# Input weights in tile slots, a second buffer for the decay factors, and reorderings in the merge, cross-attention and second feed-forward product of a hybrid decoder block

## The chip, the cores and the metric

The kernel runs on one core of a Trainium2 chip. The metric is the device time of one execution in microseconds. A core has a matmul engine (PE, with a queue of its own for loading weights, PEld), a vector engine (DVE), a scalar engine (ACT), a third elementwise engine (POOL), a queue that issues most DMAs (SP) and 16 DMA engines that these transfers share. Each engine carries out its own list of instructions strictly in order and waits on semaphores for the others; an instruction that waits holds up everything behind it on its engine.

## The reference, cut to what matters

```python
u = rms_norm(x, norm_mix)                                  # 1024 tokens x 1024
u_ssm, q, k, v, f, gates = split(u @ w_in)
y  = gelu(s5_ssm(u_ssm, lam_re, lam_im, log_dt, b_re, b_im, c_re, c_im, d_skip))
a, b = split(y @ w_glu);  out_a = a * sigmoid(b)
out_b = forgetting_attention(q, k, v, f + b_forget) @ w_fox_o
ga, gb = split(sigmoid(gates))
h = x + (ga * out_a + gb * out_b) @ w_mix_out              # the merge of the branches
h = h + memory_cross_attention(rms_norm(h), rms_norm(mem), w_mem_q, w_mem_kv, w_mem_o)
fa, fb = split(rms_norm(h) @ w_ffn_in)                     # 2 x 2816 columns
h = h + (silu(fa) * fb) @ w_ffn_out
return rms_norm(h, norm_final)

def s5_ssm(u, ...):                                        # 32 groups x 64 complex states
    dt = exp(log_dt);  lam_bar = exp(lam * dt);  b_bar = (lam_bar - 1) / lam * b
    states = scan(s[t] = lam_bar * s[t-1] + b_bar @ u[t])
    return real(c @ states) + d_skip * u
```

All inputs and results are float32.

## The kernel before, in words

**Precision and tiles.** Every float32 operand of a matmul is split into a high part (an ACT cast, `A.copy`, line 178) and a low part (a subtraction on DVE or POOL, line 179); a product is three matmuls of high and low parts (lines 168 to 170). Tiles have 128 partitions. An accumulator occupies a bank: there are tags `mm`, `sc`, `pv` and `misc`, and `misc` has one buffer, so whoever fills it next waits until the one before has been read by both the ACT cast and the DVE subtraction.

**stage_in.** The x tiles (0 to 7) and the memory tiles (m, n) are loaded into 11 slots of the tag `xt`, normalised, turned by PE through banks misc and pv (line 226), and split on the way out (`E` steps; `uh`, `ul` for x). Weights are loaded (`D`, line 388), split (`W`) and used: W0 to W3 are keys, W4 to W7 values, W8 to W11 (written 8, 9, a, b in the table) the 512 columns of the input projection for the state-space branch (`U`), whose splits also rearrange columns. The order is the table `ORDER_IN`, one step after the other; within it a scheduler places every engine's instructions, so the lists of the engines are not simply the table cut in five. Raw weights have 4 slots. The keys and values (`kv`) are stored to `kv_d` right after they are made (lines 412 and 427), and the projected columns to `u_d` (line 439).

**stage_ssm.** The 16 column blocks of the gates (24 matmuls for each half, then a sigmoid on ACT, line 475, and a store) fill PE while DVE, POOL and ACT prepare the state-space products of four quarters q. Per quarter: POOL and DVE build tables (`w`, `Gm`, the doubled rotations `EC`, `ES`); ACT copies the decay factors into `r` (line 1354); DVE runs two scans with `r` (lines 1414 and 1415, `zre` and `zim`); a Toeplitz table `Ts` is completed by three DMAs that shift it (line 1378) and copied to `Tt` (line 1383); PE then multiplies `Tt` and the states `St` (lines 1442 and 1443). Gate weights come two blocks at a time, p = 0 to 7, each as two 512 KB loads (`raw`, line 153).

**Merge.** `fox_part` multiplies the attention by `w_fox_o` into pv banks, multiplies by gate `gb` (line 538) and adds; the result is split and goes through `w_mix_out` (`mix`).

**Cross-attention.** For each half of the heads and block of tokens: `mem_scores` (scores, exponent, normalising on POOL, `pe`, line 697), `mem_turn` (PE turns the probabilities, line 706), `mem_values`. `mem_turn` of one block follows the scores of the next.

**Feed-forward.** Both products use a scheme with seven products of half-size blocks instead of eight (names A11, A12, A22, S1 to S4). The first runs over 22 column blocks j: `start`, `middle`, `end` are PE work (line 878), `w_first`, `w_sums` and `w_last` split the weights; `middle` ends with an ACT copy `c` (line 899) of bank mm, which PE needs next for S4. The second product reads operands of 128 x 1024 (`or`), fetched and split by `o_get` seven steps ahead of `o_mm`; the first few are split while the last block of the first product runs.

**Order.** `with B.behind(i)` puts the instructions in its body behind instruction `i` in the list of their own engines; it adds no wait between engines.

Of the kernel before, what the change touches and what calls it, by code (L numbers as in the profile page):

```python
# [66 lines left out]
def f32(ap):  # L67
    return ap.bitcast(F32)
# [50 lines left out]
class Block:  # L119
# [57 lines left out]
    def split(self, hi, lo, src, pool_lo=False):  # L177
        self.A.copy(hi, src)  # L178
        (self.G if pool_lo else self.V).tensor_sub(lo, src, f32(hi))  # L179

    def rstd(self, src):
# [47 lines left out]
    def turned(self, ps, b, act, t):  # L229
        for i in range(0, 4, act.kg):  # L230
            hi, lo = act.tok(4 * b + i, t, act.kg)
            self.split(hi, lo, ps[:, i * P:(i + act.kg) * P].rearrange("p (k c) -> p k c", k=act.kg))

# [104 lines left out]
def stage_in(B, xp, s5, x, mem, g_mix, g_kv, w_in, w_mem_kv, uT, u_d, kv_d):  # L338
# [7 lines left out]
    mT = Act(xp, "mT", 4, 8, ML, kg=4, name="m")  # L346
    tiles, gain, ss, rs, raw, w, ps, us, kv = {}, {}, {}, {}, {}, {}, {}, [], []
    names = {"m": -2, "n": -1, **{str(t): t for t in range(NT)}}
# [28 lines left out]
    def evac(t, b):  # L377
        B.turned(ps.pop((t, b)), b, *((mT, t + 2) if t < 0 else (uT, t)))

    def wget(i):  # L380
        if i < 4:
            src = w_mem_kv[:, i * P:(i + 1) * P]
        elif i < 8:
            src = w_mem_kv[2 * (i - 4) * P:2 * (i - 3) * P, 512:1024]
        else:
            src = w_in[:, C_U + (i - 8) * P:C_U + (i - 7) * P]
        raw[i] = B.wpool.tile([P, RAW], F32, tag="raw", bufs=4, name="raw")[:, :D]
        S.dma_start(raw[i].rearrange("p (k c) -> p k c", k=D // src.shape[-1]),
                    src.rearrange("(k p) c -> p k c", p=P))
# [15 lines left out]
    def keys_out(h):  # L405
        if not kv:
            kv.extend(xp.tile([P, D], F32R, tag="kv", bufs=4, name="kv") for _ in range(4))
        cs = slice(h * ML, (h + 1) * ML)
        B.split(kv[0][:, cs], kv[1][:, cs], ps.pop(("k", h))[:, :ML])
        if h == 3:  # L410
            for i in range(2):
                S.dma_start(kv_d[i], f32(kv[i]))

# [8 lines left out]
    def values_out():  # L422
        for t in range(2):
            cs = slice(t * 512, (t + 1) * 512)
            B.split(kv[2][:, cs], kv[3][:, cs], ps.pop(("v", t)))
        for i in range(2, 4):
            S.dma_start(kv_d[i], f32(kv[i]))
# [5 lines left out]
    def ssm_out(q, h):  # L433
# [4 lines left out]
        if h == 1:  # L438
# [9 lines left out]
            "K": lambda a: keys(int(a)), "k": lambda a: keys_out(int(a)), "V": lambda a: values(int(a)),  # L448
            "v": lambda a: values_out(), "U": lambda a: ssm_in(int(a[0]), int(a[1])),
            "u": lambda a: ssm_out(int(a[0]), int(a[1])), "L": lambda a: s5.load(int(a)),  # L450
# [5 lines left out]
def stage_ssm(B, s5, qp, uT, w_in, gate_d, u_d, y_d):  # L456
# [5 lines left out]
    def gate_weights(p):  # L462

        w[p] = [B.wblock(w_in, 4 * n, 4, C_G + 256 * p, 256) for n in range(2)]

# [38 lines left out]
def stage_tail(B, big, s2, sh, x, glu, aT, gate_d, kv_d, w_fox_o, w_mix_out, g_mq, w_mem_q, w_mem_o, g_ffn,  # L504
# [21 lines left out]
    def fox_part(j):  # L526
# [6 lines left out]
        for h in range(2):  # L533
            cs = slice(512 * h, 512 * h + 512)
            po = B.bank("pv")
            B.gemm_t(po, fh[:, :, o:o + P], fl[:, :, o:o + P], aT, h, 4)
            gb = load(gate_d[D + j * P:D + (j + 1) * P, cs], "gb")
            V.tensor_mul(gb, gb, po)
# [62 lines left out]
    def ahead(j):  # L601
# [14 lines left out]
        def plain():  # L616
            hl, _ = pair(0)
            B.split(*hl, pre[j][0])
            for i, t_ in enumerate(hl):
# [114 lines left out]
    def cross(hf):  # L734
        steps = [(b, tt) for b in range(2) for tt in range(4)]
        fs = []
        for i in range(len(steps) + 1):
            if i < len(steps):
                fs.append(lambda s=steps[i]: mem_scores(hf, *s))
            if i > 0:  # L740
                fs.append(lambda s=steps[i - 1]: mem_turn(hf, *s))
                if steps[i - 1][1] == 3:
                    fs.append(lambda b=steps[i - 1][0]: mem_values(hf, b))
        return fs
# [94 lines left out]

    def w_sums(j):  # L840
        b_, e_ = wpair(j), slot(F32R, "we")
# [48 lines left out]
    def middle(j):  # L890
# [7 lines left out]
        c1 = ev[j, "c1"] = sh.half("c1")  # L898
        A.copy(c1, b1)
        V.scalar_tensor_tensor(out=c1, in0=c1, scalar=-1.0, in1=b3, op0=ALU.mult, op1=ALU.subtract)  # L900

    def end(j):
# [69 lines left out]
    w_last(1)  # L972
    middle(1)
    w_sums(2)
    out_fetch(0, w_fetch(3).ins)
    for j in range(2, NF):
# [14 lines left out]

    LAST, AHEAD = 4, 7
    ORDER = (1, 2, 6, 7, 5, 4, 3)
# [76 lines left out]
    for m, (n, p) in enumerate(seq):  # L1070
        if n == 3 and p >= NP - LAST:
            break
        for i in range(4):
            o_mm(m, i)
        if m + AHEAD < len(seq):
            o_get(m + AHEAD)
# [68 lines left out]
class S5:  # L1145
# [5 lines left out]
    def __init__(self, B, sp, lam_re, lam_im, log_dt, b_re, b_im, c_re, c_im, d_skip):  # L1151
        self.B, self.sp = B, sp
        self.raw = (lam_re, lam_im, log_dt, b_re, b_im, c_re, c_im, d_skip)
        self.xgs = {}

# [140 lines left out]
    def weights(self, q):  # L1296
# [61 lines left out]
    def turn_weights(self, q):  # L1358
# [18 lines left out]
        for n in (1, 2, 4):  # L1377
            S.dma_start(self.Ts[0:P - 16 * n, 8 - 2 * n:8 - n], self.Ts[16 * n:P, 8 - n:8])

# [474 lines left out]
```

## Time and profile before

| | |
|---|---|
| runs (median of 3) | 1574.35 us (1570.27 to 1576.2) |
| profiled execution | 1572.18 us, span of its instructions 1570.4 us |
| DVE, ACT, POOL busy | 1024.0, 658.6, 265.1 us |
| mean granted clock of PE | 0.991 |
| DMA | 235.09 MB, 150 GB/s over the span |

All times in the views are counted from the start of the span. A row of a timeline has the start, the duration, the engine and line, what is written and read, and in brackets the idle time ahead of it on its engine and what ended that. A row of the windows has, for PE, PEld, DVE, ACT and POOL, the busy time and number of instructions, then the granted clock of PE as a share of full speed, the mean busy share of the DMA engines and GB/s.

### The profile page before, as it was taken

Reading aid. Unit: us, or ns where it says so; the run is one execution under the profiler, and the core shown is the slowest. Engines: PE = TensorE matmul, PEld = TensorE weight load, DVE = VectorE, ACT = ScalarE, POOL = GpSimd, SP = SyncE. Lnnn points to the kernel's source line nnn. Section 1 sums busy time; section 2 is a strip of 40 time slices with the busy share of each in tenths; the row PEclk is TensorE's granted clock in tenths of the full one; section 3 lists DMA queues with packets and bytes.
Section 4 is the critical chain, followed back from the end, with each engine's and each line's share of the span. In section 5 each row is a group of like instructions: output and inputs, shape, how many; then the busy total and the mean of one; then the engine's idle time right before and its main releaser. Section 6 shows DMA issues by size and latency. Waiting matters only on the chain.

```text
span 1570.4 us, 20364 instructions
## 1 busy us (share of the span) xinstructions
PE 1529.5 (97%) x7313; PEld 1259.6 (80%) x7313; DVE 1024.0 (65%) x1822; ACT 658.6 (42%) x1177; POOL 265.1 (17%) x343
## 2 busy tenths in 40 slices
PE   7899999999999999999999999999999999999997
PEld 6688888898777678878888787888888888788886
DVE  6746555444688877685555698777777775566555
ACT  6422434323566753232435564333333332354342
POOL 3026653200112124110002200000000000001001
PEclk8999999999999999999999999999999999999999
DMA  8753456332034556378310256554555543896642
GB/s 295 154 108 94 129 100 150 100 130 30 16 68 91 136 151 208 102 227 282 121 54 14 90 195 188 171 161 155 161 161 160 161 148 134 277 391 218 195 153 108
DMA packets 196101, 235.09 MB, mean 150 GB/s; under 512 B 35144, under 2 KB 127208, under 8 KB 195488
## 3 DMA queue, kind: packets, MB, share of 16 engines
q1 hardware_dynamic: 188512, 215.97, 46.9%
q10 hardware_dynamic: 7488, 17.83, 3.0%
q8 instruction: 57, 0.93, 0.2%
q14 instruction: 44, 0.36, 0.1%
HBM read 162.98 MB, written 72.71 MB: 150 GB/s over the span
## 4 chain that ended last, share of the span: by engine, by line
PE 81%; DVE 8%; DMA 4%; ACT 3%; POOL 2%; issue 2%; SPq 0%; POOLq 0%; ACTq 0%; DVEq 0%
PE mm L878 14%; PE mm L168 8%; PE mm L170 8%; PE mm L169 8%; PE pv L878 7%; PE mm L1018 5%; PE sc L878 4%; PE sc L1018 4%; PE sc L168 3%; PE sc L170 3%; PE sc L169 3%; PE pv L1018 3%; PE misc L1018 2%; DMA raw<-in_w_in_dram 1%; DMA raw<-in_w_mem_kv_dram 1%
## 5 line engine op out<-in xcount | busy, mean ns | idle before, releaser
L178 ACT CAST whi<-raw 128x1024 fp32r<-128x1024 f32 (+2 forms) x123 | 114.8, 940 | 170.9 <-PE mm L878 52.8
L179 DVE TENSOR_TENSOR wlo<-raw,whi 128x1024 fp32r<-128x1024 f32 (+2 forms) x120 | 128.6, 1078 | 66.5 <-ACT whi L178 64.6
L168 PE MATMUL mm<-uh,whi 128*128 128x512 f32 x344 | 136.5, 397 | 0.1
L179 DVE TENSOR_TENSOR ol<-or,oh 128x1024 fp32r<-128x1024 f32 x73 | 92.2, 1267 | 67.5 <-ACT oh L178 66.6
L169 PE MATMUL mm<-ul,whi 128*128 128x512 f32 x344 | 134.8, 392 | 0.0
L170 PE MATMUL mm<-uh,wlo 128*128 128x512 f32 x344 | 134.6, 392 | 0.0
L178 ACT CAST oh<-or 128x1024 fp32r<-128x1024 f32 x73 | 76.8, 1053 | 103.4 <-PE mm L1018 33.3
L910 POOL TENSOR_TENSOR g<-a,c 128x512 f32<-128x512 f32 x22 | 35.8, 1627 | 387.3 <-ACT a L909 280.9
L1668 POOL TENSOR_TENSOR pl<-pf,ph 128x512 fp32r<-128x512 f32 (+1 forms) x32 | 37.8, 1182 | 236.1 <-DVE ph L1667 195.9
L170 PEld LDWEIGHTS mm<-uh,wlo 128*128 128x128 f32 x344 | 64.6, 188 | 13.6 <-DVE wlo L179 0.5
L168 PEld LDWEIGHTS mm<-uh,whi 128*128 128x128 f32 x344 | 64.8, 188 | 11.9 <-DVE mc L1633 0.4
L169 PEld LDWEIGHTS mm<-ul,whi 128*128 128x128 f32 x344 | 64.8, 188 | 11.1
L197 POOL TENSOR_TENSOR r<-ms,mhalf 128x1 f32<-128x1 f32 (+1 forms) x30 | 19.4, 649 | 307.3 <-DVE ms L193 279.8
L1665 ACT ACTIVATE pf<-sc 128x512 f32<-128x512 f32 (+1 forms) x96 | 46.5, 490 | 44.0 <-DVE sc L1661 28.1
L878 PE MATMUL pv<-S3h,we 128*128 128x512 f32 x176 | 57.8, 389 | 0.0
L1671 DVE TENSOR_TENSOR pl<-pf,ph 128x512 fp32r<-128x512 f32 (+2 forms) x64 | 35.1, 549 | 11.3 <-ACT ph L1670 10.7
L1134 POOL TENSOR_TENSOR sg<-sg,ga 128x512 f32<-128x512 f32 x16 | 30.1, 1905 | 73.0 <-DVE sg L1127 52.4
L178 ACT CAST we<-rawb 128x512 fp32r<-128x512 f32 x20 | 12.5, 624 | 69.1 <-PE pv L878 37.0
L1018 PE MATMUL mm<-oh 128*128 128x512 f32 x106 | 41.2, 389 | 0.0
L1018 PE MATMUL mm<-ol,oh 128*128 128x512 f32 x106 | 41.2, 389 | 0.0
L1018 PE MATMUL mm<-oh,ol 128*128 128x512 f32 x106 | 41.2, 389 | 0.0
L168 PE MATMUL sc<-uh,whi 128*128 128x512 f32 x104 | 40.8, 393 | 0.0
(583 smaller groups left out, 4593.0 us busy)
## 6 DMA issues: line engine op xcount, KB each, us to landing
or<-c_d SPq DMA_DIRECT2D x77, 256.0 KB
raw<-in_w_in_dram SPq DMA_DIRECT2D x22, 512.0 KB
wo<-in_w_ffn_out_dram SPq DMA_DIRECT2D x22, 512.0 KB
c_d<-g SPq DMA_DIRECT2D x44, 256.0 KB
t_d<-wo SPq DMA_DIRECT2D x44, 256.0 KB
or<-t_d SPq DMA_DIRECT2D x44, 256.0 KB
rawb<-in_w_ffn_in_dram SPq DMA_DIRECT2D x20, 512.0 KB
raw<-in_w_ffn_in_dram SPq DMA_DIRECT2D x20, 512.0 KB
```

Of the source, the lines that this page charges most:

```text
L168: T.matmul(ps, lh, rh, start=first, stop=False)
L169: T.matmul(ps, lh, rl, start=False, stop=False)
L170: T.matmul(ps, ll, rh, start=False, stop=last)
L178: self.A.copy(hi, src)
L179: (self.G if pool_lo else self.V).tensor_sub(lo, src, f32(hi))
L878: T.matmul(ps, l_[:, k, :], r_, start=first and k == 0 and i == 0, stop=k == 3 and i == 2, skip_group_check=True)
L910: G.tensor_mul(g[:, 512:], a1, c1)
L1018: T.matmul(ps, l_[:, gi], r_[:, 512:], start=n < 3 and p == 0 and k == 0 or n == 7 and p == 0 and k == 0, stop=p == NP - 1 and k == 2, ski ...
L1134: self.B.G.tensor_mul(self.out[j][:, cs], self.out[j][:, cs], ga)
L1665: self.exp = A.activation(pf[:, off:], ps[:, off:], AF.Exp)
L1668: G.tensor_sub(pl[:, off:], pf[:, off:], f32(ph[:, off:]))
L1671: V.tensor_sub(pl[:, off:], pf[:, off:], f32(ph[:, off:]))
```

## The change

The change computes the same with the same operations on the same tiles; it changes where some tiles live, how many buffers one of them has, which engine makes one low part, and the order.

1. Input projection: W8, W9 and W10 are loaded into `xt` slots (`xw`) that memory tiles m and n and x tile 1 had, ahead of all stores; W11 stays in a raw slot; the casts of W8 to W11 stand behind the cast of the latest bank that was read (`casts[-1]`). The stores of keys and values get steps of their own (y0, y1). W11's low part is made on DVE instead of POOL.
2. State-space stage: `r` has two buffers; the gate weights of odd p stand behind the last shift of `Ts`.
3. Merge: `fox_part` takes banks pv, pv, misc in turn; the casts of the second mixing weight, and of the feed-forward weights made ahead of time, stand behind the last split of the merge.
4. Cross-attention: `mem_turn` follows the scores two blocks later instead of one.
5. Feed-forward: casts of the next weights stand behind the copy `c`, and most operands of the second product behind the last `c`.

```diff
@@ ORDER_IN, second to last lines
-E11 D7 Q5 T20 R2 T21 E21 E20 S4 E30 W6 D8 W7 T40 V1 D9 S5 E40 T31 V2 E31 W8 T41 L0 V3 Da T50 Q6 v T51 W9
-E51 U00 Db Q7 E41 R3 S6 u00 L1 Wa T60 E50 S7 T61 T70 Wbg E61 U10 E60 T71 E70 E71 P0 U20 u10 u20 P1 U21 U11 U30
+E11 D7 D8 D9 Da Q5 T20 R2 T21 E21 E20 S4 E30 W6 Db L0 W7 T40 V1 S5 E40 T31 V2 E31 W8 T41 V3 y0 E41 W9 T50 Q6 v T51 E51
+U00 Q7 R3 S6 u00 L1 T60 E50 S7 Wa T61 T70 E61 Wb U10 E60 T71 E70 E71 P0 y1 U20 u10 u20 P1 U21 U11 U30
@@ stage_in
-        B.turned(ps.pop((t, b)), b, *((mT, t + 2) if t < 0 else (uT, t)))
+        casts.append(B.turned(ps.pop((t, b)), b, *((mT, t + 2) if t < 0 else (uT, t))))
...
-        raw[i] = B.wpool.tile([P, RAW], F32, tag="raw", bufs=4, name="raw")[:, :D]
+        raw[i] = xtile("xw") if 8 <= i < 11 else B.wpool.tile([P, RAW], F32, tag="raw", bufs=4, name="raw")[:, :D]
...
-            B.split(*[t_.rearrange("p (k n g) -> p k n g", k=8, n=16) for t_ in hl],
-                    raw.pop(i).rearrange("p (k g n) -> p k n g", k=8, g=8), pool)
+            with B.behind(casts[-1]):
+                B.split(*[t_.rearrange("p (k n g) -> p k n g", k=8, n=16) for t_ in hl],
+                        raw.pop(i).rearrange("p (k g n) -> p k n g", k=8, g=8), pool)
...
+    def kv_store(n):
+        for i in (2 * n, 2 * n + 1):
             S.dma_start(kv_d[i], f32(kv[i]))
@@ stage_ssm
-        w[p] = [B.wblock(w_in, 4 * n, 4, C_G + 256 * p, 256) for n in range(2)]
+        with B.behind(s5.shifted if p % 2 else None):
+            w[p] = [B.wblock(w_in, 4 * n, 4, C_G + 256 * p, 256) for n in range(2)]
@@ the merge
-            po = B.bank("pv")
+            po = B.bank(("pv", "pv", "misc")[(2 * j + h) % 3])
...
-            B.split(mh, ml, sg[:, cs])
+            merged.append(B.split(mh, ml, sg[:, cs]))
...
-    wm1 = mix_weights(1)
+    with B.behind(merged[-1]):
+        wm1 = mix_weights(1)
@@ cross
-            if i > 0:
-                fs.append(lambda s=steps[i - 1]: mem_turn(hf, *s))
+            if i > 1:
+                fs.append(lambda s=steps[i - 2]: mem_turn(hf, *s))
@@ feed-forward
-        B.split(*wts[j, 6], ra[:, :512])
+        with B.behind(copied):
+            B.split(*wts[j, 6], ra[:, :512])
...
-        middle(j)
+        ahead_of, copied = copied, middle(j)
         if j + 1 < NF:
-            w_first(j + 1)
-            w_sums(j + 1)
+            with B.behind(ahead_of):
+                w_first(j + 1)
+                w_sums(j + 1)
...
-    for m in range(4):
+    for m in range(3):
         o_get(m)
+    with B.behind(copied):
+        for m in range(3, 8):
+            o_get(m)
     end(NF - 1)
-    for m in range(4, AHEAD):
-        o_get(m)
+    with B.behind(copied):
+        o_get(8)
@@ class S5
-        r8 = t2("r8")
+        r8 = t2("r8", 2)
...
-            S.dma_start(self.Ts[0:P - 16 * n, 8 - 2 * n:8 - n], self.Ts[16 * n:P, 8 - n:8])
+            self.shifted = S.dma_start(self.Ts[0:P - 16 * n, 8 - 2 * n:8 - n], self.Ts[16 * n:P, 8 - n:8])
```

**Where the instructions stand.** First SP in the input projection: before, two stores of keys (`kv_d`) lie between the last value weight (`in_w_mem_kv`) and W8 and W9.

```order
L388 DMA raw_448<-in_w_mem_kv_dram 128x2x512
L412 DMA kv_d_83<-kv_296 128x1024
L412 DMA kv_d_83<-kv_297 128x1024
L388 DMA raw_486<-in_w_in_dram 128x8x128
L388 DMA raw_509<-in_w_in_dram 128x8x128
L1167 DMA prow_546<-in_lam_re_dram 16x128
```

The same place of SP after the change, with W8 to W10 in `xw` and W11 in `raw_490`.

```order
L390 DMA raw_446<-in_w_mem_kv_dram 128x2x512
L390 DMA xw_448<-in_w_in_dram 128x8x128
L390 DMA xw_450<-in_w_in_dram 128x8x128
L390 DMA xw_452<-in_w_in_dram 128x8x128
L390 DMA raw_490<-in_w_in_dram 128x8x128
L1179 DMA prow_492<-in_lam_re_dram 16x128
```

The stores have moved behind the parameters of the state-space branch, and all four weights of the projection stand together.

ACT round the cast of W8 (`whi_537`), before: two reads of banks of tile 4 (`uh1` of misc_451, `uh3`) stand behind the cast.

```order
L178 CAST uh0_0_87<-misc_451 128x2x128
L178 CAST uh2_0_91<-pv_516 128x2x128
L178 CAST whi_537<-raw_486 128x1024
L178 CAST uh1_0_89<-misc_451 128x2x128
L178 CAST uh3_0_93<-pv_516 128x2x128
L178 CAST whi_599<-raw_509 128x1024
```

After, W8's cast is `whi_560`.

```order
L178 CAST uh0_0_87<-misc_455 128x2x128
L178 CAST uh2_0_91<-pv_539 128x2x128
L178 CAST uh1_0_89<-misc_455 128x2x128
L178 CAST uh3_0_93<-pv_539 128x2x128
L178 CAST whi_560<-xw_448 128x1024
L178 CAST uh0_1_88<-misc_517 128x2x128
```

Both reads have moved ahead of the cast.

SP at the end of the projection and in the first quarter of the state-space stage, before: a gate weight (`raw`) stands behind each of the last stores of u (`u_d`), and two more ahead of the shifts of `Ts`.

```order
L439 DMA u_d_77<-us_967 128x8x128
L153 DMA raw_1612<-in_w_in_dram 128x4x256
L439 DMA u_d_77<-us_648 128x8x128
L153 DMA raw_1618<-in_w_in_dram 128x4x256
L1388 DMA xg_1224<-u_d_77 128x1024
L1388 DMA xg_1552<-u_d_77 128x1024
L153 DMA raw_1940<-in_w_in_dram 128x4x256
L153 DMA raw_1946<-in_w_in_dram 128x4x256
L1378 DMA Ts_1332<-Ts_1332 112x128
L1378 DMA Ts_1332<-Ts_1332 96x256
L1378 DMA Ts_1332<-Ts_1332 64x512
```

After:

```order
L441 DMA u_d_77<-us_967 128x8x128
L441 DMA u_d_77<-us_646 128x8x128
L1400 DMA xg_1224<-u_d_77 128x1024
L1400 DMA xg_1552<-u_d_77 128x1024
L1390 DMA Ts_1332<-Ts_1332 112x128
L1390 DMA Ts_1332<-Ts_1332 96x256
L1390 DMA Ts_1332<-Ts_1332 64x512
L153 DMA raw_1612<-in_w_in_dram 128x4x256
L153 DMA raw_1618<-in_w_in_dram 128x4x256
L153 DMA raw_1940<-in_w_in_dram 128x4x256
L153 DMA raw_1946<-in_w_in_dram 128x4x256
```

All four gate weights now stand behind the shifts.

ACT there, before (`r8_1521` belongs to the second quarter, `Tt_1610` to the first):

```order
L475 ACTIVATE gs_1549<-sc_1524 128x512
L1354 COPY r8_1521<-R_805 128x512
L476 DMA gate_d_79<-gs_1549 128x512
L475 ACTIVATE gs_1579<-mm_1554 128x512
L476 DMA gate_d_79<-gs_1579 128x512
L178 CAST whi_1614<-raw_1612 128x1024
L178 CAST whi_1620<-raw_1618 128x1024
L475 ACTIVATE gs_1607<-sc_1582 128x512
L1383 COPY Tt_1610<-Ts_1332 128x8x8x16
```

After (`r8_1937` belongs to the third quarter; the copy for the second has moved up behind that for the first):

```order
L478 ACTIVATE gs_1549<-sc_1524 128x512
L1366 COPY r8_1937<-R_803 128x512
L479 DMA gate_d_79<-gs_1549 128x512
L478 ACTIVATE gs_1579<-mm_1554 128x512
L479 DMA gate_d_79<-gs_1579 128x512
L178 CAST whi_1614<-raw_1612 128x1024
L178 CAST whi_1620<-raw_1618 128x1024
L478 ACTIVATE gs_1607<-sc_1582 128x512
L1395 COPY Tt_1610<-Ts_1332 128x8x8x16
```

Only the buffer of the `r` copy has changed its number at this place.

ACT at the end of the first feed-forward product, before (`oh` are operands of the second product, `c1_11992` is the last copy `c`):

```order
L895 COPY a1_11966<-mm_11884 128x512
L178 CAST oh_12064<-or_12061 128x1024
L178 CAST oh_12071<-or_12068 128x1024
L899 COPY c1_11992<-mm_11884 128x512
L178 CAST whi_12024<-or_12021 128x1024
```

After:

```order
L902 COPY a1_11966<-mm_11884 128x512
L906 COPY c1_11992<-mm_11884 128x512
L178 CAST whi_12024<-or_12021 128x1024
L178 CAST oh_12031<-or_12028 128x1024
L178 CAST oh_12038<-or_12035 128x1024
```

The copy has moved ahead of the two casts.

More of the change, by code (lines that the diff above doesn't have):

```diff
@@ L177, in split @@
     def split(self, hi, lo, src, pool_lo=False):
-        self.A.copy(hi, src)
+        cast = self.A.copy(hi, src)
         (self.G if pool_lo else self.V).tensor_sub(lo, src, f32(hi))
+        return cast
     def rstd(self, src):
@@ L231, in turned @@
             hi, lo = act.tok(4 * b + i, t, act.kg)
-            self.split(hi, lo, ps[:, i * P:(i + act.kg) * P].rearrange("p (k c) -> p k c", k=act.kg))
+            cast = self.split(hi, lo, ps[:, i * P:(i + act.kg) * P].rearrange("p (k c) -> p k c", k=act.kg))
+        return cast
     def norm_turn(self, xs, act, t):
@@ L346, in stage_in @@
     mT = Act(xp, "mT", 4, 8, ML, kg=4, name="m")
-    tiles, gain, ss, rs, raw, w, ps, us, kv = {}, {}, {}, {}, {}, {}, {}, [], []
+    tiles, gain, ss, rs, raw, w, ps, us, kv, casts = {}, {}, {}, {}, {}, {}, {}, [], [], []
     names = {"m": -2, "n": -1, **{str(t): t for t in range(NT)}}
@@ L409, in keys_out @@
         B.split(kv[0][:, cs], kv[1][:, cs], ps.pop(("k", h))[:, :ML])
-        if h == 3:
-            for i in range(2):
-                S.dma_start(kv_d[i], f32(kv[i]))
     def values(kk):
@@ L656, in stage_tail @@
     wm0 = mix_weights(0)
-    wm1 = mix_weights(1)
+    with B.behind(merged[-1]):
+        wm1 = mix_weights(1)
     mixes = [lambda t=t: mix(t, 0, wm0) for t in range(NT)] + [lambda t=t: mix(t, 1, wm1) for t in range(4)]
@@ L898, in middle @@
         c1 = ev[j, "c1"] = sh.half("c1")
-        A.copy(c1, b1)
+        copied = A.copy(c1, b1)
         V.scalar_tensor_tensor(out=c1, in0=c1, scalar=-1.0, in1=b3, op0=ALU.mult, op1=ALU.subtract)
+        return copied
     def end(j):
@@ L972, in stage_tail @@
     w_last(1)
-    middle(1)
-    w_sums(2)
+    copied = middle(1)
+    w_sums(2, copied)
     out_fetch(0, w_fetch(3).ins)
@@ L989, in stage_tail @@
             gated(j // 2 - 1)
[L992 removed]
+    LAST, AHEAD, EARLY = 4, 7, 9
     ORDER = (1, 2, 6, 7, 5, 4, 3)
```

18 lines of the change are left out of this document (9 added, 9 removed).

## The prediction

> **What bounds the kernel now.** I read the page first, then the waits of the matmul engine, then 4 us windows round its two largest waits, then the timelines of the engines at those places.
>
> ```profile
> PE 1529.5 (97%) x7313; PEld 1259.6 (80%) x7313; DVE 1024.0 (65%) x1822; ACT 658.6 (42%) x1177; POOL 265.1 (17%) x343
> PE 81%; DVE 8%; DMA 4%; ACT 3%; POOL 2%; issue 2%; SPq 0%; POOLq 0%; ACTq 0%; DVEq 0%
> 1000.00:1050.00 50.00, 50.00 (x222) 41.43 (x221) 33.11 (x46) 17.61 (x28) 3.22 (x2) 1.00 0.50 156
> ```
>
> The matmul engine (PE) is busy for 1529.5 of 1570.4 us. In the feed-forward loop (the window of 50 us) it is busy all the time at clock 1.00, one matmul every 50/222 = 0.225 us, and the program has the same 7313 matmuls after the change. So nothing can be won there; only PE's waits and its slow clock can go. 1570.4 - 1529.5 = 41 us is all the idle time, lead-in and tail with it.
>
> ```profile
> PE misc L226 <- DVE ul L179: 6.9, 2, 5.4
> PE mm L878 <- ACT c L899: 2.1, 2, 1.4
> PE pv L1442 <- ACT Tt L1383: 1.8, 1, 1.8
> PE misc L706 <- POOL pe L697: 1.3, 4, 0.5
> PE misc L706 <- DVE ptl L179: 1.1, 1, 1.1
> PE pv L168 <- DVE gb L538: 0.8, 2, 0.4
> ```
>
> These are the waits at the places that the change touches (total, times, longest): input projection 6.9, second half of the feed-forward 2.1, state-space merge of the first quarter 1.8, cross-attention 2.4, branch merge 0.8. Together 14.0 us. The clock adds to them (last columns of the windows: clock, DMA share, GB/s):
>
> ```profile
> 48.00:52.00 4.00, 0.73 (x4) 0.77 (x5) 3.12 (x4) 3.23 (x4) 0.00 (x0) 0.76 0.19 42
> 52.00:56.00 4.00, 4.00 (x12) 3.14 (x11) 3.94 (x7) 1.23 (x3) 0.00 (x0) 0.50 1.02 134
> 56.00:60.00 4.00, 4.00 (x21) 3.32 (x20) 2.69 (x8) 2.48 (x7) 0.00 (x0) 0.88 1.03 194
> 160.00:164.00 4.00, 2.49 (x16) 2.46 (x17) 2.14 (x4) 3.24 (x5) 3.37 (x13) 0.84 0.37 135
> 164.00:168.00 4.00, 4.00 (x23) 3.82 (x23) 0.00 (x0) 1.42 (x3) 3.30 (x15) 0.73 0.00 0
> ```
>
> If the clock is either full or half, a mean of 0.76 over 4 us is 2 x 0.24 x 4 = 1.9 us of half; the first three windows hold 1.9 + 4.0 + 1.0 = 6.9 us, of which PE works some 5.6 (it starts again at 51.27, below), which costs 5.6/2 = 2.8. The other two hold 1.3 + 2.2 = 3.5, which costs 1.7. So the wait of 5.4 really costs 8.2, and that of 1.8 costs 3.5.
>
> **Part 1, input projection.** This is what stands behind the wait of 5.4:
>
> ```profile
> 35.20 0.94 SPq L412 DMA_DIRECT2D kv_d<-kv  x2
> 36.19 2.65 SPq L388 DMA_DIRECT2D raw<-in_w_in_dram  x2
> 46.94 1.91 ACT L178 CAST whi<-raw 128x1024 fp32r<-128x1024 f32 x1 [4.17 <-DMA raw<-in_w_in_dram]
> 48.75 0.36 ACT L178 CAST uh<-misc 128x256 fp32r<-128x256 f32 x1
> 50.70 0.42 DVE L179 TENSOR_TENSOR ul<-misc,uh 128x256 fp32r<-128x256 f32 x1
> 51.27 1.09 PE L226 MATMUL misc<-ident,xt 128*128 128x128 f32 x4 [5.38 <-DVE ul L179]
> ```
>
> SP issues the first weight (W8) at 36.19, behind two stores of keys that had to wait for the keys. It lands at 46.9; ACT stands at its cast, and the two reads of the misc bank (uh, then ul) are queued behind it. PE needs that bank at 45.9. After the change three of the weights go into slots of x tiles that are free once PE has turned the tiles, and SP issues them ahead of every store; W8's cast also stands behind the last reads of the banks of tile 4, so no bank is held by it. **The whole cause of the 5.4 goes, and the 2.8 with it.** The second wait of this kind has the same cause with W11:
>
> ```profile
> 68.76 1.95 ACT L178 CAST whi<-raw 128x1024 fp32r<-128x1024 f32 x1 [0.64 <-DMA raw<-in_w_in_dram]
> 71.01 0.42 DVE L179 TENSOR_TENSOR ul<-misc,uh 128x256 fp32r<-128x256 f32 x1 [1.17 <-ACT uh L178]
> 71.58 0.63 PE L226 MATMUL misc<-ident,xt 128*128 128x128 f32 x4 [1.55 <-DVE ul L179]
> 70.84 2.90 POOL L179 TENSOR_TENSOR wlo<-raw,whi 128x1024 fp32r<-128x1024 f32 x1 [26.64 <-ACT whi L178]
> ```
>
> So 5.4 + 2.8 + 1.55 = 9.75 us stand here. Not all of it goes. What is late next is the misc bank again: it has one buffer, and the long pieces of the four weights (1.91 to 1.95 on ACT, about the same on DVE for the low part, W11's now on DVE as well instead of 2.90 on POOL) still have to be put between short reads of that bank. Each can cost what W11 did, 1.55. I see room for three such waits (behind W8's, W9's and W10's low parts, round the turns of the state-space parameters and of the last x tile): 3 x 1.5 = 4.5. Bounds: none of the three, -9.75; all three and after each a slow stretch like that after 161.5 (1.7 each), 9.75 - 4.5 - 5.1, -0.2. I take 9.75 - 4.5 = **-5.2**, in the middle. The four stores of keys now come last in this queue; only cross-attention, hundreds of us later, reads them, so their lateness costs nothing.
>
> [...]
>
> **Part 2, state-space stage, first quarter.**
>
> ```profile
> 107.60 0.37 SPq L439 DMA_DIRECT2D u_d<-us  x1
> 108.38 0.37 SPq L153 DMA_DIRECT2D raw<-in_w_in_dram  x1
> 108.00:116.00 8.00, 8.00 (x37) 6.64 (x36) 0.35 (x1) 1.98 (x3) 3.10 (x6) 1.00 1.05 141
> 92.00:95.00 3.00, 3.00 (x15) 2.48 (x14) 2.86 (x6) 0.00 (x0) 1.51 (x2) 1.00 1.03 273
> 116.25 0.11 POOL L1422 MEMSET St<- 128x8 f32 x1 [5.00 <-DMA u_d<-us]
> 131.65 1.06 DVE L1346 TENSOR_TENSOR d<-EC,trg_cs 128x128 f32<-128x128 f32 x1 [2.19 <-POOL ES L1348]
> 145.26 9.52 SPq L1378 DMA_DIRECT2D Ts<-Ts  x3
> 156.52 0.62 ACT L1354 COPY r<-R 128x512 f32<-128x512 f32 x1 [12.51 <-DVE zim L1415]
> 158.03 1.99 ACT L178 CAST whi<-raw 128x1024 fp32r<-128x1024 f32 x2 [0.40 <-ACT gs L475]
> 160.42 1.03 ACT L1383 COPY Tt<-Ts 128x1024 f32<-128x1024 f32 x1
> 161.51 0.49 PE L1442 MATMUL pv<-xg,Tt 128*128 128x128 f32 x2 [1.82 <-ACT Tt L1383]
> ```
>
> PE waits for the Tt copy; ACT makes it late, because it stood 12.51 us at the copy of the decay factors (r), until the scans of this quarter had read the only buffer. **The second buffer by itself does not free ACT**: the order shows the copy of the third quarter standing where that of the second stood, and it waits for the same scans. What does help is less plain. The scans end a chain that begins at 116.25, where POOL waits for the last store of u. That store shares 108 to 116 with a 512 KB gate weight (141 GB/s x 8 us = 1.13 MB, both). The weight is now issued after the shifts of Ts, so the store runs alone: at the rate of 92 to 95 (273 GB/s) it would land at about 110.5, by half the 8 us at about 112. From 116.25 POOL works on these tables until DVE can take over at 131.65, and DVE goes on to the scans. POOL's idle time before it is 5.00, so the chain can start 4 to 5 us sooner; I take 4. Then r goes at 152.5 and Tt, 3.9 after it as now, at 156.4, ahead of PE's 159.7. The shifts of Ts go out with two gate weights less ahead of them, at 141.3, and the two gate weights behind them; if the shifts keep 9.5 us, the weights issue at 150.8 and, 1 MB at 141 GB/s, land at 158.2, two casts (1.99), gs and Tt follow, and PE waits for 1.8 as before. If the two weights ahead of them (1 MB) made up most of the 9.5, they land at 153 to 155 and nothing waits. So the bounds are 0 and -3.5, and +4.2 if the chain does not start sooner either (the shifts end at 154.8, the weights land at 162.2, and ACT is at their casts at 158.0). I take **-3.5**, as the 1.05 DMA share says that the queues, not the shifts, were what was slow.
>
> **Part 3, the rest.** Third bank in the branch merge: the two waits for gb (0.8) go, since PE has a bank more before it needs gb's read to be over; the casts of the second mixing weight now stand behind the merge, with eight mixes of 24 matmuls (8 x 24 x 0.225 = 43 us) as cover; without it, a cast and its low part (1.04 for a cast of that size, the row of 1345.59 below, and the low part taken as long): -0.8 to +2.1, I take **-0.7**. Cross-attention: the turn of a probability block comes one block later, so 2.4 of waits (the longest 1.1) have one block of scores more as cover; at the end of each row of blocks there is no next block, and I leave a third standing: 0 to -2.4, I take **-1.5**. Feed-forward:
>
> ```profile
> 969.51 0.58 ACT L899 COPY c<-mm 128x512 f32<-128x512 f32 x1
> 1345.59 1.04 ACT L178 CAST oh<-or 128x1024 fp32r<-128x1024 f32 x1 [4.60 <-DMA or<-in_w_ffn_out_dram]
> 1346.54 0.58 ACT L899 COPY c<-mm 128x512 f32<-128x512 f32 x1
> 1020.34 0.62 ACT L178 CAST whi<-raw 128x512 fp32r<-128x512 f32 x1 [4.57 <-PE mm L878]
> 1020.87 0.58 ACT L899 COPY c<-mm 128x512 f32<-128x512 f32 x1
> ```
>
> At 1346.54 the copy that frees a bank stands behind a cast that waited 4.60 for its DMA; now the copy goes first and the casts of the second product behind it, and the same at 969.51 with the sixth weight. Of 2.1 I take **-1.8** (0 to -2.1). Within the loop cast and copy change places as in the last two rows; PE has no wait there to lose, and the cover is a cast that starts 0.6 later on an engine busy 17.6 of 50 us.
>
> Sum: -5.2 - 3.5 - 0.7 - 1.5 - 1.8 = -12.7. The profiled execution is 1572.18 (span 1570.4), so 1559.5; it lies 2.2 under the median of 1574.35, where the same sum gives **1561.6**.
>
> **Rivals.** (a) *Part 2 stays as it is* (ACT still blocked at r, or the gate weights late): 1565. For it: the r copy stands where it stood. 0.18. (b) *The misc bank takes back the gain of part 1*, by three waits with slow clock: 1566.6; the loss of both (a) and (b), 1570. For it the 1.55 at 71.58, against it that this 1.55 brought no slow stretch. 0.16 for (b), 0.05 for both. (c) *No new waits in part 1*: 1557. 0.13. (d) *Slower*: in the loop of the feed-forward the casts of the next step now wait behind the copy c, 20 times. If PE catches each by the 0.62 of the cast and the low part behind it (0.69, as long), 20 x 1.3 = 26 us come on. It decides from 12.7/20 = 0.64 us a step on; at 1.05 a step the time is 1582.6. Against it: the loop has no wait at all now, and ACT is idle two thirds of it. 0.05. (e) *The slow stretch after 161.5 does not come from the wait of 1.82* and stays when that goes: 1.7 less of gain, 1563.3. For it, the 1.55 at 71.58 brought none. 0.05. [...] My forecast has the rest, 0.38.
>
> **Range and chances.** From 1555.5 (every wait of the table and both slow stretches gone, 14.0 + 4.5, with the median's base) to 1571 (both (a) and (b), with 1 us for the spread of the runs, as the low end has 0.4). A measurement of this kernel tells about 0.5%, 7.9 us, from no change: 1566.5. Forecast, (c), (e) and most of (a) lie beyond it, (b) at the edge: faster 0.68, within 0.26, slower 0.06.
>
> **What would show it.** In the profile after: no wait of PE over 2 us between 40 and 75, and no clock under 0.9 there; waits for misc of 1 to 2 us, if (b). POOL's wait for u_d gone or under 2 us; the shifts under 7 us; PE without a wait for Tt, clock 1.00 at 150 to 165. No wait of mm L878 for c. It is wrong if PE waits for x turns in the first 50 us, or if waits appear inside the loop.

## The result, and the profile after

| | before | after |
|---|---|---|
| median (runs) | 1573.98 us (6; 1570.27 to 1576.2) | 1565.77 us (6; 1564.7 to 1567.56) |
| ratio, 95% interval | | 0.9949 (0.9936 to 0.9963) |
| profiled execution, span | 1572.18, 1570.4 us | 1567.56, 1565.8 us |

The change makes the kernel 0.5% faster, 8.2 us by the medians; 12.7 were forecast, 1561.6, in a range of 1555.5 to 1571. The two profiled executions differ by only 4.6, since that of before is below its median and that of after is the slowest of its six.

The page of the changed kernel, busy times and the chain; then PE's waits at the places that the change touches (total, times, longest).

```profile
PE 1526.9 (98%) x7313; PEld 1260.8 (81%) x7313; DVE 1015.4 (65%) x1823; ACT 661.1 (42%) x1177; POOL 264.7 (17%) x342
PE 84%; DVE 6%; DMA 3%; ACT 2%; issue 2%; POOL 1%; SPq 0%; POOLq 0%; DVEq 0%; ACTq 0%
...
PE pv L1454 <- ACT Tt L1395: 7.3, 1, 7.3
PE misc L1200 <- issue: 3.0, 1, 3.0
PE misc L227 <- DVE edt_p L260: 1.5, 1, 1.5
PE misc L712 <- POOL pe L703: 0.5, 1, 0.5
PE misc L712 <- DVE ptl L179: 0.2, 1, 0.2
```

The waits for c and for gb no longer appear; of cross-attention's 2.4, 0.7 are left; the input projection's 6.9 have become 4.5 in two waits. One wait grew: PE now stands 7.3 us for `Tt` instead of 1.8. The windows of the changed kernel show what each of these did to the clock (third column from the right).

```profile
48.00:52.00 4.00, 3.66 (x21) 2.88 (x20) 3.37 (x8) 3.19 (x5) 0.00 (x0) 1.00 0.25 50
52.00:56.00 4.00, 3.27 (x15) 2.38 (x13) 3.19 (x4) 1.33 (x4) 0.00 (x0) 1.00 1.00 167
...
158.00:162.00 4.00, 0.00 (x0) 0.00 (x0) 2.46 (x4) 1.57 (x3) 3.18 (x8) 0.69 0.30 103
162.00:166.00 4.00, 3.99 (x18) 3.99 (x19) 3.83 (x10) 1.91 (x3) 0.84 (x1) 0.50 0.34 124
```

The slow stretch of 50 to 57 is gone; one as long now follows the wait for `Tt`.

PE's list has the same 7313 matmuls in both kernels, so the start of the n-th can be set side by side. Differences to before in us (minus is earlier), over stretches of the list, one profiled execution each; the columns besides the changed kernel are experiments told of below:

| stretch (matmul number, time before) | changed | e2 early pair | e5 part 1 alone | e6 parts 3 to 5 alone |
|---|---|---|---|---|
| to 400 (95.9): input projection | -5.0 | -5.5 | -4.8 | +3.2 |
| 400 to 750 (170.8): Tt, first quarter | +5.8 | -3.9 | -2.6 | -2.4 |
| 750 to 3300 (672.1): state space, attention | +1.6 | -0.9 | +0.9 | +4.5 |
| 3300 to 3900 (805.3): merge | -1.5 | -1.5 | +0.3 | -1.5 |
| 3900 to 4350 (893.2): cross-attention | -2.5 | -2.7 | +0.3 | -2.6 |
| 4350 to 6300: first feed-forward product | -1.0 | -1.0 | -0.1 | -1.0 |
| 6300 to 6500: start of the second product | -1.6 | -1.6 | +2.8 | -1.6 |

So parts 1 and 3 to 5 gained 11.6, and the place of `Tt` gave 5.8 of it back. The 1.6 between 750 and 3300 is a slow stretch in the attention that the execution before does not have (clock 0.72 in 557 to 563, against 1.00); the change touches nothing there. How far one execution is from another shows where nothing was edited: e6 has the input projection of before and ends it 3.2 us later; e5 and e6 have the order of before at the place of `Tt` and are 2.6 and 2.4 us faster there than the execution of before; the +2.8 of e5 in the last row goes with a slow stretch at 1342. A difference of 2 or 3 us in a row of this table can be chance, unless several kernels repeat it, as they do in the rows of the merge, cross-attention and the feed-forward products.

What made `Tt` late, from the timelines of the changed kernel:

```profile
102.46 1.14 ACT L1366 COPY r<-R 128x512 f32<-128x512 f32 x2
106.16 0.11 POOL L1434 MEMSET St<- 128x8 f32 x1
134.16 4.81 SPq L1390 DMA_DIRECT2D Ts<-Ts  x3
139.01 4.82 SPq L153 DMA_DIRECT2D raw<-in_w_in_dram  x4
140.00:152.00 12.00, 12.00 (x54) 9.94 (x53) 10.68 (x16) 2.16 (x3) 5.09 (x7) 1.00 1.00 90
146.54 0.62 ACT L1366 COPY r<-R 128x512 f32<-128x512 f32 x1 [7.52 <-DVE zim L1427]
146.62 0.33 ACTq L479 DMA_DIRECT2D gate_d<-gs  x1
153.38 1.05 ACT L178 CAST whi<-raw 128x1024 fp32r<-128x1024 f32 x1 [2.98 <-DMA raw<-in_w_in_dram]
160.43 0.60 ACT L478 ACTIVATE gs<-sc 128x512 f32<-128x512 f32 x1 [5.99 <-DMA gate_d<-gs]
160.92 1.04 ACT L1395 COPY Tt<-Ts 128x1024 f32<-128x1024 f32 x1
162.01 0.80 PE L1454 MATMUL pv<-xg,Tt 128*128 128x128 f32 x2 [7.31 <-ACT Tt L1395]
```

Up to 146.6 this is what was forecast: POOL no longer waits for the store of u (no bracket at 106.16), the shifts take 4.8 instead of 9.5, and the scans let r go 10 us earlier. Then four gate weights, 2 MB, issued at 139 to 144, fill the DMA engines (share 1.00, 90 GB/s). A store of gates issued by ACT at 146.62 is queued behind them: the first packet of ACT's queue moves at 153.4, while in stretches without loads it follows the issue by 0.8 us. With two buffers of `gs` ACT cannot write the next until the store has landed, at 160.4. `Tt`, whose data had been complete for some 20 us, stands behind that. The gates of this store had been ready since 139.0; in ACT's list its issue stands behind the copy of `r`, which waited 7.52 for the scans. Issuing the store ahead of that copy was not tried.

### The profile page after: what moved, and what is told of

Same layout as the page of the kernel before. It is cut to its first block, busy times and chain, and to the rows that moved or that the text cites. A ratio compares the mean times of both kernels' runs of the same rounds, so it can differ in the third digit from the quotient of the medians.

```text
span 1565.8 us, 20345 instructions
## 1 busy us (share of the span) xinstructions
PE 1526.9 (98%) x7313; PEld 1260.8 (81%) x7313; DVE 1015.4 (65%) x1823; ACT 661.1 (42%) x1177; POOL 264.7 (17%) x342
## 4 chain that ended last, share of the span: by engine, by line
PE 84%; DVE 6%; DMA 3%; ACT 2%; issue 2%; POOL 1%; SPq 0%; POOLq 0%; DVEq 0%; ACTq 0%
PE mm L885 15%; PE mm L168 8%; PE mm L170 8%; PE mm L169 8%; PE pv L885 8%; PE mm L1027 5%; PE sc L1027 4%; PE sc L885 4%; PE sc L168 3%; PE sc L169 3%; PE sc L170 3%; PE pv L1027 3%; PE misc L1027 2%; PE pv L168 1%; DMA gate_d<-gs 1%
## 5 line engine op out<-in xcount | busy, mean ns | idle before, releaser
L178 ACT CAST whi<-raw 128x1024 fp32r<-128x1024 f32 (+2 forms) x120 | 109.5, 915 | 116.4 <-PE mm L169 48.4
L907 DVE SCALAR_TENSOR_TENSOR c<-c,pv 128x512 f32<-128x512 f32 x22 | 15.1, 688 | 78.0 <-ACT c L906 77.8
L168 PE MATMUL mm<-yh,whi 128*128 128x512 f32 x104 | 41.3, 397 | 0.0
```

Of the source, the lines that this page charges most:

```text
L168: T.matmul(ps, lh, rh, start=first, stop=False)
L178: cast = self.A.copy(hi, src)
```

## The experiments

**e1: a third buffer for gs.** The decay factors give up their second buffer for it.

```diff
-        gs = qp.tile([P, 512], F32, tag="gs", bufs=2, name="gs")
+        gs = qp.tile([P, 512], F32, tag="gs", bufs=3, name="gs")
-        r8 = t2("r8", 2)
+        r8 = t2("r8")
```

> The changed kernel, but three buffers for the sigmoids of the gates (gs) instead of two, and to make room one buffer for the decay factors as before the change. In the changed kernel PE waits 7.31 us for the Tt copy; ahead of that copy ACT waits 5.99 us to write gs, because the stores of both gs buffers are queued behind 2 MB of gate weights. Theory A (the gate stores behind the weights hold ACT): the wait for a store goes; the later of the two casts still waits for its weight until 153.4, so Tt is done at about 156 and PE waits about 1.3 us instead of 7.3; no or a shorter slow stretch; 6 to 9 us faster than the changed kernel (1557 to 1560). Theory B (the weights themselves are late, the store only came last): PE waits 5 us or more, time as the changed kernel within 2 us. Theory C (the second buffer of the decay factors is needed): the scans or r come later and PE waits longer.

Measured: 1561.32 us, ratio 0.9925 (0.9912 to 0.9937), some 4 us faster than the changed kernel. ACT and PE's wait in this kernel:

```profile
153.41 1.05 ACT L178 CAST whi<-raw 128x1024 fp32r<-128x1024 f32 x1 [3.17 <-DMA raw<-in_w_in_dram]
154.36 0.59 ACT L478 ACTIVATE gs<-sc 128x512 f32<-128x512 f32 x1
154.85 1.03 ACT L1395 COPY Tt<-Ts 128x1024 f32<-128x1024 f32 x1
...
PE pv L1454 <- ACT Tt L1395: 1.5, 1, 1.5
```

The weight lands when it did (153.4), the wait for the store is gone, and PE's wait falls from 7.3 to 1.5, as theory A has it. B and C fall: the weights themselves account for the 1.5, and one buffer of decay factors does no harm. Between matmuls 400 and 750 this kernel is 7.9 us better than the changed one (-2.1 against +5.8). The 4 us by the medians fall short of the 6 to 9 expected; in its profiled execution part of the 7.9 is lost again between 750 and 3300, where nothing was edited.

**e2: the pair p = 3 early.** It goes behind the loads `xg`, when the DMA engines stand nearly idle (share 0.00 to 0.23 between 112 and 136 in the changed kernel); the pair p = 4 stays behind the shifts of the first quarter.

```diff
-        with B.behind(s5.shifted if p % 2 else None):
+        with B.behind(s5.fetched if p == 3 else s5.shifts[2] if p == 4 else s5.shifted if p % 2 else None):
             w[p] = [B.wblock(w_in, 4 * n, 4, C_G + 256 * p, 256) for n in range(2)]
...
```

> The changed kernel, but the pair of gate weights p = 3 is issued behind the loads xg (when the DMA engines stand idle, 112 to 138 us in the changed kernel's trace) instead of behind the shifts of Ts; the pair p = 4 stays behind the shifts. Only SP's list changes. Theory A: 1 MB instead of 2 MB lies ahead of the gate stores, and the casts find their weight at once; PE's wait for Tt falls from 7.3 to below 0.5 us, no slow stretch there, POOL's start and the shifts stay as early as in the changed kernel; 8 to 10 us faster than the changed kernel (1556 to 1558). Theory B: the same. Rival (the DMA engines carry any load this slowly here, 80 to 100 GB/s): the gate stores still take until 155, PE waits 1 to 3 us.

Measured: 1557.51 us, 0.9906 (0.9891 to 0.9922). SP, then ACT, in this kernel:

```profile
106.81 0.93 SPq L153 DMA_DIRECT2D raw<-in_w_in_dram  x2
139.69 1.14 SPq L153 DMA_DIRECT2D raw<-in_w_in_dram  x2
...
147.99 2.00 ACT L178 CAST whi<-raw 128x1024 fp32r<-128x1024 f32 x2 [0.40 <-ACT gs L478]
149.90 0.59 ACT L478 ACTIVATE gs<-sc 128x512 f32<-128x512 f32 x1
150.38 1.04 ACT L1396 COPY Tt<-Ts 128x1024 f32<-128x1024 f32 x1
```

No wait for a store or a weight stands ahead of `Tt`, which is done 2.4 us before PE wants it; PE has no wait there and no slow stretch. This place is 3.9 us better than before the change instead of 5.8 worse. By the medians it is 7 to 8 us faster than the changed kernel, at the lower edge of what was expected. Stores of gates are held up by the pair p = 3 here too (ACT waits 5.43 for one at 117.72), but there PE is not waiting for ACT.

**e3: no gate weights behind the shifts.**

```diff
-        with B.behind(s5.shifted if p % 2 else None):
+        with B.behind(None):
```

> The changed kernel, but the odd gate weights are not put behind the shifts of Ts; SP's list there is that of before the change. Theory A: what the change did at this place is undone on both sides: POOL waits again for the last store of u, 4 us or more, the shifts take 8 us or more again, and PE waits 1 to 2.5 us for Tt, with a slow stretch of some 3 us. 5 to 6 us faster than the changed kernel (1560 to 1561). If it is not faster, the putting behind is not what costs.

Measured: 1558.08 us, 0.9909 (0.9896 to 0.9922), 6 to 8 us faster than the changed kernel, a little more than expected, and not to be told from e2. The first row below is POOL's, the others SP's, ACT's and PE's.

```profile
109.69 0.11 POOL L1434 MEMSET St<- 128x8 f32 x1 [4.12 <-DMA u_d<-us]
138.71 9.58 SPq L1390 DMA_DIRECT2D Ts<-Ts  x3
149.97 0.62 ACT L1366 COPY r<-R 128x512 f32<-128x512 f32 x1 [11.64 <-DVE zim L1427]
154.96 0.49 PE L1454 MATMUL pv<-xg,Tt 128*128 128x128 f32 x2 [0.94 <-ACT Tt L1395]
```

Everything is as late again as before the change (4.1 us for the store of u, 9.6 for the shifts, 11.6 at r), and still PE waits only 0.94, without a slow stretch: ACT finds its weights and stores done. So the chain behind the store of u, which the putting behind does shorten, costs PE no more than that 0.94 once the rest of the change is in; what the putting behind costs is the crowding. Without that one edit the change is worth 14.8 us instead of 8.2; part 1 alone (e5) and parts 3 to 5 alone (e6) add up to the same, 6.7 + 8.2 = 14.9.

**e4: one buffer for the decay factors.**

> The changed kernel, but one buffer for the decay factors. The lists of all engines stay as they are but for the buffer of r that is copied at each place. Theory A: no change, within 1.5 us of the changed kernel (1564 to 1567), PE's wait for Tt 7.3 within 0.5. Theory C (the second buffer frees ACT or POOL somewhere): slower by 2 us or more.

The edit is the second half of e1's. Measured: 1565.35 us, 0.9958 (0.9945 to 0.997), against 0.9949 for the changed kernel: no difference in time. PE's wait for `Tt` is 6.4, a little less than expected, and is split otherwise: the weight landed only at 155.1 and the wait for the store was 2.76 instead of 5.99. The second buffer gains nothing that shows. Against this kernel e1 has the third buffer of `gs` and no other difference: 4.0 us faster, measured together.

**e5: part 1 alone**, the rest as before the change.

> The kernel before with part 1 of the change alone (input projection: weights in x slots, casts behind the banks, stores of keys and values later, the last low part on DVE). By the changed kernel's trace part 1 is worth 5.0 us at matmul 400 (95.87 to 90.86). Theory A (the loss is all in the order of the gate weights, which this kernel has as before): the 5.0 stand, and PE's wait for Tt is 0.9 to 1.8 us as in the unpinned kernel: 5 to 8 us faster than before, 1565 to 1568. Theory D (an earlier end of the input projection by itself makes Tt late, since the chain behind the last store of u does not move with it): PE waits over 5 us for Tt and nothing is gained.

Measured: 1567.32 us, 0.9954 (0.9939 to 0.9968), 6.7 faster than before. Theory A holds: 4.8 us at matmul 400, and PE waits 0.87 for `Tt` with no slow stretch. D falls; the chain behind the store of u moves with the projection.

**e6: parts 3 to 5 alone.**

> The kernel before with parts 3 to 5 alone (merge, cross-attention, feed-forward). The prediction had 4.0 us for them (0.7 + 1.5 + 1.8). By the changed kernel's trace, matmul for matmul, they are worth 1.5 + 2.5 + 1.0 + 1.6 = 6.6 us. Theory A: 5 to 7.5 us faster than before, 1565.5 to 1568. Theory E (these edits only shift waits, and the trace's 6.6 is an accident of phase): 2 us or less.

Measured: 1565.75 us, 0.9949 (0.9931 to 0.9967), 8.2 faster, a little more than the 5 to 7.5 expected. In its profile (table above) the edited stretches are worth 6.7, the same in all three kernels that have them, to 0.2 each. Theory E falls. Its profiled execution also shows how much the old input projection can vary by itself:

```profile
51.77 1.09 PE L227 MATMUL misc<-ident,xt 128*128 128x128 f32 x4 [6.01 <-DVE ul L179]
73.47 1.09 PE L227 MATMUL misc<-ident,xt 128*128 128x128 f32 x4 [3.17 <-DVE ul L179]
```

These were 5.38 and 1.55 in the profile of before. Also, PE waits 1.1 for `Tt` here instead of 1.82, and no slow stretch is counted between 160 and 170, with nothing of the change at that place.

**e7: the product dbc on POOL**, from e2's kernel.

```diff
-        V.tensor_tensor(out=self.dm, in0=self.dm,
+        G.tensor_tensor(out=self.dm, in0=self.dm,
```

> The kernel of the early pair, with the product dbc (skip weights by a mask) on POOL instead of DVE; only these two lists change, by that one instruction. In the changed kernel PE waits 3.03 us for the misc bank at 58.30, 2.26 in the kernel of the early pair, where the reads of that bank stand behind this product on DVE, which waits 1.64 for the landing of dbc. Theory A: that wait shrinks by the 1.6 to below 1.5 us, 1 to 2 us faster than the kernel of the early pair (1555.5 to 1556.5). Theory F (the cast of W10 and its low part, 1.9 each, set that wait): no change within 0.7 us.

Measured: 1557.62 us, 0.9893 (0.9878 to 0.9909), not to be told from e2. PE's waits in the input projection of this kernel:

```profile
56.16 0.23 PE L1200 MATMUL misc<-ident,prow 48*128 48x48 f32 x1 [0.92 <-PE mm L170]
59.66 0.44 PE L1207 MATMUL misc<-ident,craw 128*128 128x128 f32 x2 [1.75 <-DVE par L1202]
66.00 0.63 PE L227 MATMUL misc<-ident,xt 128*128 128x128 f32 x4 [1.50 <-DVE edt_p L260]
```

The first fell from 2.26 to 0.92 as theory A has it, but two others of 1.75 and 1.50 now follow, where e2 has 0.63 and a slow stretch (3.4 long, 1.7 lost); matmul 400 stands within 0.1 us of e2's. The loss was moved, not removed.

**e8: the casts not put behind the banks**, from e2's kernel.

```diff
-            with B.behind(casts[-1]):
+            with B.behind(None):
```

> The kernel of the early pair without putting the casts of W8 to W11 behind the reads of the banks. The weights are loaded as early as there, so a cast need not wait for its load. Theory A (the 5.38 us before the change were the late load; the place of the cast matters little once the load is early): within 1.5 us of the kernel of the early pair. Theory G (a cast of 1.9 us ahead of a read of the misc bank costs PE as long each time, whatever its load does): one to three waits for misc of 1 to 2 us more, 2 to 5 us slower.

Measured: 1556.97 us, 0.9888 (0.9872 to 0.9905), not to be told from e2. Its waits are others:

```profile
47.63 0.63 PE L227 MATMUL misc<-ident,xt 128*128 128x128 f32 x4 [2.33 <-DVE ul L179]
52.76 0.63 PE L227 MATMUL misc<-ident,xt 128*128 128x128 f32 x4 [1.27 <-DVE ul L179]
61.61 0.44 PE L1207 MATMUL misc<-ident,craw 128*128 128x128 f32 x2 [0.35 <-DVE cT_re L1208]
```

Two waits of 2.3 and 1.3 us come, much as theory G has it, but e2's 2.26 and its slow stretch go, and the time is A's. With the load early, where the cast stands matters little.

**e9 and e10: low parts on POOL**, W11's alone (as before the change), and W10's and W11's, both from e2's kernel (`Wb` to `Wbg`, `Wa` to `Wag` in the table of steps).

> The kernel of the early pair with W11's low part on POOL again, as before the change. Taken off DVE: 1.95 us. Theory H (after the change DVE's long low parts are what PE waits for in the input projection; the wait goes where DVE is late, as it moved and did not shrink when dbc was taken off): the waits for misc between 55 and 70, 2.3 + 0.6 in the kernel of the early pair and 3.0 + 1.5 in the changed kernel, fall by 0.6 to 1.5, matmul 400 stands at 88.9 to 90 instead of 90.4; total 1556 to 1557.5. Rival (POOL's low part takes 2.9 and slows DVE's small operations, as before the change): no gain, or 1 us slower.

> The same with the low parts of W10 and W11 on POOL. Taken off DVE: 3.9 us. Theory H: the waits in the input projection fall below 1.5 us in all, matmul 400 at 88 to 89.5, total 1554.5 to 1556.5. Rival: POOL's 2.9 each makes W10 late for its matmuls, and PE waits for wlo instead: total 1557 to 1560.

Measured: 1559.25 us, 0.9917 (0.9902 to 0.9931), and 1560.55 us, 0.992 (0.9904 to 0.9936): not faster than e2's 1557.51. The intervals overlap with e2's, so that they are slower isn't shown; in the profiles matmul 400 stands 3.7 and 3.0 us later than in e2, of which up to 1.7 go in each with more time at half clock. Theory H falls. Of the rivals, e9's holds; e10's time is just above its range, but PE never waits there for a low part that POOL made. POOL and DVE in e9, and the same DVE operations in e2:

```profile
62.57 2.88 POOL L179 TENSOR_TENSOR wlo<-raw,whi 128x1024 fp32r<-128x1024 f32 x1 [18.64 <-ACT whi L178]
62.67 2.81 DVE L256 SCALAR_TENSOR_TENSOR edt_r<-edt_k,edt_xc 128x16 f32<-128x16 f32 x1
```

```profile
62.40 1.95 DVE L179 TENSOR_TENSOR wlo<-raw,whi 128x1024 fp32r<-128x1024 f32 x1
64.26 0.18 DVE L256 SCALAR_TENSOR_TENSOR edt_r<-edt_k,edt_xc 128x16 f32<-128x16 f32 x1
```

While POOL makes the low part, a DVE operation on 128 x 16 elements, 0.18 us in e2, takes 2.81: it ends with POOL's. Taking 1.95 us off DVE cost it 2.6. In e10 two such operations take 2.37 and 2.00, and each again ends with POOL's. So moving W11's low part to DVE cost nothing that shows; that it is a part of the change that gains is likely, but not clear of the spread.

## Why the prediction was right or wrong

**Direction and range** held; 8.2 us came of 12.7. The size is near the rival "part 2 stays as it is" (1565), but not for its reason alone: part 2 lost instead of staying, and parts 3 to 5 gained more. That the total lies so near is partly luck: in the profiles part 2 missed its term by 9.3 us and part 3 of the sum by 2.6 the other way.

**Part 1 was right in mechanism, and its size agrees as far as it can be told**: -5.2 forecast, -5.0 measured (-4.8 alone, e5). Against e6's execution of the old projection it would be some 8. The 5.38 and the slow stretch went, and short waits took their place, 3.03 and 1.48 and two of 0.3 and 0.2, against the 4.5 that were put down, with no slow stretch in the changed kernel. Two details were wrong: the one of 3.03 did not come from a low part alone, since the reads of the bank stood behind a product that waited for a parameter's load, yet taking that away did not shorten the sum (e7); and the place of the cast, told as half the cause, does not matter (e8). That leaves the early load, which the changed kernel shows as forecast; the second row is W8's cast, without a wait:

```profile
28.37 5.55 SPq L390 DMA_DIRECT2D xw<-in_w_in_dram  x3
43.38 2.01 ACT L178 CAST whi<-xw 128x1024 fp32r<-128x1024 f32 x1
```

SP issued the first of these weights at 36.19 before. No run keeps the late load with the rest of part 1, so what the new order of steps and stores round it adds is not told apart.

**Part 2 was wrong, and this is the step that failed:** "they land at 153 to 155 and nothing waits". Its earlier links all held: POOL's wait for the store of u, the shorter shifts (4.8), r freed 10 us earlier (5 of them by part 1), no use in the second buffer (e4), and the second weight that the casts need did land at 153.4. But something waited. The sum had "the two gate weights behind them", and four follow the shifts, as SP's list showed: 2 MB. And it followed the loads to their casts only, not to the other traffic on the same DMA engines: the stores of gates that ACT issues, whose landing frees the two buffers of gs. Of the 7.3, 5.8 go with a third buffer (e1); the other 1.5 are the weight itself, in e1's execution. The bound of +4.2 on this place was worked out with the same omission, and +5.8 lies outside it. With 1 MB taken out of the way this place shows -3.9 (e2) where -3.5 was forecast, but that is luck for the most part: the kernels whose SP list is the old one here show -2.4 to -2.6 (e3, e5, e6), so only some 1.3 of it go with the edit, and by the medians e2 cannot be told from e3. The rest is that the execution of before was slow here.

**Part 3 was right in mechanism and too small**: -4.0 forecast (0.7 + 1.5 + 1.8), -6.6 measured (1.5 + 2.5 + 2.6), 6.7 in e6. In each the wait of the table went, or most of it, and 0.5 to 0.8 us more besides. The forecast had left a third of cross-attention's waits standing, rightly (0.7 of 2.4), and took the listed waits for all there was. Where the rest comes from (shorter delays than are listed as waits, perhaps) was not tried.

**The rivals.** (d), a loss in the feed-forward loop, did not show: the difference stays at -2.58 from matmul 5000 to 6300. (e), that the slow stretch after 161.5 does not hang on the wait of 1.82, is left half open: e6 has the same lists there, a wait of 1.1 and no slow stretch, and -2.4 at this place without any edit. So most of the 3.5 that was to be won could come and go by chance.

## What to carry to other kernels

A load that is moved can take the DMA engines from whatever else is on them, as the gate weights did here (share 1.00 from 140 to 152; the store issued at 146.62 moved at 153.4): before moving one, list the stores and loads of every queue in the stretch it lands in, and ask which buffer each of them frees and what stands behind its next writer. Count the bytes behind a new order edge from the instruction list, not from the edit, and look up how long each of these loads took in the profile, since equal loads did not take equal time here (below). And where DVE or a one-buffer bank is what PE waits for, removing one wait can shift it to the next reader (e7, e8); compare the start of a later matmul, not the wait. Compare it also with a kernel that was not edited at that place, since one execution can be 2 or 3 us off by itself.

## What the runs showed of the hardware that was not expected

**The slow stretches of PE's clock had two lengths here.** Summing 1 us windows, every stretch of half clock between 30 and 1540 us in these twelve kernels is 3.4 or 6.8 us long, to 0.1. Within one execution all changes of the clock lie whole multiples of 3.413 us apart, to 0.02 (e6: half clock from 48.90 to 55.72, 72.78 to 76.20, 376.58 to 379.98 and 560.90 to 564.30). What starts a stretch is not the length of a wait alone: 7.31 (after), 6.01 (e6) and 5.38 (before) each had 6.8; 2.26 (e2) and 1.73 (e1) had 3.4, 3.03 (after) and 2.33 (e8) had none. Two waits of 0.81 and 0.62, ending one us apart, come ahead of 366 in e8 as in e2, and only in e8 does a slow stretch follow (e8 first, then e2):

```profile
366.00:370.00 4.00, 4.00 (x11) 3.20 (x12) 2.25 (x7) 0.00 (x0) 0.00 (x0) 0.58 0.00 0
```

```profile
366.00:370.00 4.00, 3.92 (x18) 3.02 (x18) 2.99 (x10) 0.00 (x0) 0.00 (x0) 1.00 0.01 2
```

In the 3.4 us right before a slow stretch PE was busy at most some 64% in all twelve traces, 56% in e8 (363.2 to 366.6). That is not all there is to it: other 3.4 us with 45 and 46% (e8 from 45.7, after from 53.7), and with some 57% in e2 (from 363.0), had no slow stretch behind them. What decides whether a short wait costs clock is not shown by these runs. At clock 0.50 a stretch of 3.4 costs PE 1.7 us where it is busy throughout, an estimate, so one or two of them more or less may be a good part of the spread between runs of one kernel.

**Gate weights load at very different rates**: 90 GB/s with the DMA engines full in the changed kernel (140 to 152), 273 in the profile of before (92 to 95, with a store of u). It goes with the pair of weights, not with the crowd. Counted off in the order of the loads, the packets of 1 KB of the pair p = 3 take some 150 to 200 ns on average in all twelve traces (183 before and after the change), wherever the pair stands: at 105 to 120 before, behind the shifts in the changed kernel, in an otherwise idle stretch in e2. Those of p = 4 take some 50 to 110 (95 before, 78 after). The two pairs in e2 (p = 3, then p = 4), with the DMA engines full or nearly:

```profile
112.00:120.00 8.00, 8.00 (x37) 6.64 (x36) 1.40 (x2) 1.26 (x3) 7.10 (x22) 1.00 1.03 100
140.00:147.00 7.00, 7.00 (x32) 5.81 (x31) 6.96 (x11) 0.52 (x1) 0.47 (x1) 1.00 0.91 157
```

So the first two of the four weights behind the shifts, not all four alike, kept the DMA engines until some 152 us in the changed kernel, and the store of gates began to move at 153.4. The rival named with e2, that any load goes this slowly at that place, falls with the second row. Why this pair is slow is not known.
